# Macaron block with chunked attention and retention: a head's transposes, values and the bias a step or two later in the order of the work

## The chip, the cores and the metric

The kernel runs on one core of one Trainium2 chip. Time is device time in microseconds (us) of one execution, from the first to the last instruction and what lies around it. A shorter time is better. A tile (also a bank, where it lies in the accumulators' memory) is a buffer of 128 partitions.

## The reference

One layer over x of 256 x 2048 (f32): a half-step SwiGLU network, two mixers in parallel that are merged by sigmoid gates, a second half-step network and a last norm.

```
x = x + 0.5 * swiglu_ffn(rmsnorm(x), w_gate, w_up, w_down)          # d_ff = 5632
h = rmsnorm(x)
q_a,k_a,v_a, q_r,k_r,v_r, g_r, gate_a,gate_r = split(h @ w_in)
att = softmax(q_a k_a' * hd**-0.5 + bias[rel]) v_a                  # 8 heads of 128, chunks of 64, causal by chunk
ret = (rotary(q_r) rotary(k_r)' * decay) v_r, rms-normed a head     # 8 heads of 128
x = x + (sigmoid(gate_a)*(att @ w_out_att) + sigmoid(gate_r)*((silu(g_r)*ret) @ w_out_ret)) @ w_out
x = x + 0.5 * swiglu_ffn(rmsnorm(x), ...);  return rmsnorm(x)
```

The chunk rule only masks here: 256 rows are four chunks, and each sees its own and those before it.

## The kernel before

Every large product is a matmul in f32r, in three terms: both operands are split into a rounded part `hi` (ACT copies, line 122) and a rest `lo` (DVE subtracts, line 123), and PE adds hi x hi, lo x hi and hi x lo (lines 130 to 132, the tiles `acc`).

**Steps.** The kernel is a list of steps. A step takes one weight tile `raw` of 256 x 512 (512 KB, loaded by SP's queue) through twelve products of 512 columns: two halves of x, two blocks of rows, three terms. (In the gated parts, which use Strassen's scheme, tiles `z...`, a step has six.) Ahead of step c the weights of up to three steps further on are split. There are four places for split weights, so the split for step c+3 can start when the products of step c-1 are done.

**Work beside the products.** All else is put in a table of due times by hand: `later(n, fn)` puts fn n steps after the one that is being recorded, `at(step, fn)` puts it at a step. In a step the recording runs the split ahead first, then what is due, in the order in which it was put in the table, then the step's products. Each engine works through its own instructions in the order of recording. So what a due function has on PE stands ahead of the step's products, and what it has on DVE stands behind a split.

**Banks.** Products accumulate in tiles `acc` and `z` (three each). Work beside them uses the two side banks; a tile takes the one whose last reader was recorded first, and waits for that reader.

**The stretch around the change** lies between the last gated step and the merge. Step `mixed`, called m here, is the first of the value projection VR1 (m to m+7); then QR0 (to m+15), KR0 (to m+23), QR1 (to m+31), KR1 (to m+39), and the output products with `w_out_att` from m+40.

- *Bias.* `set_bias` at m-6 loads the relative bias, transposed, from a table in memory (`biasT`, two DMAs on POOL's queue). Four steps later, at m-2, `bias_natural` turns it on PE in four groups of four transposes (`psb`, line 326), each into a side bank and copied out by ACT (`bias`, line 331).
- *Attention*, head h, from m+4+4h: **scores** (PE `as`, lines 854 and 855; DVE adds the bias into `p`, line 862, and takes the maxima `m`), a step later **powers** (ACT's exponentials, line 876), in the third step **shares** (DVE divides, line 884), in the fourth **transposes** (PE `apt`, line 890, copied by ACT), and in the sixth **values** (PE `av`, lines 898 and 899; ACT copies `atth`, DVE subtracts `attl`, line 344). Each head shifts by four steps, so that the sixth step of one is the second of the next.
- *Retention's operands.* After QR0, KR0, QR1 and KR1, ACT copies the result out, DVE applies the rotary turn to its two halves in the first and second step after (`qr00r`, `qr01r` and so on, lines 815 to 818), and in the fourth PE transposes them (`qr0p`, `kr0p`, `qr1p`, `kr1p`, line 349) for ACT and DVE to copy (`qr0T` ...).
- *Retention*, heads 0 to 3 after KR0 and 4 to 7 after KR1: `RET_WAIT` steps after the projection the first head's **scores** (PE `rs`, lines 923 and 924; DVE multiplies by the decay, `rp`, lines 926 and 927), the next head's two steps later; **values** (PE `ro`, lines 936 to 938) two steps behind a head's scores; and behind the fourth head's values **finish** (ACT squares, DVE sums `ms`, POOL's power `rs`, DVE scales `rg`, line 954). Three steps later `ret.put` transposes the result (`retp`).
- *Merge.* The gates come back from memory as `siga` and `sigr` (POOL's queue, line 1010); DVE multiplies them with the output products (line 1027).

## Time and profile before

| | |
|---|---|
| median of 3 runs (lowest to highest) | 2120.16 us (2119.79 to 2121.63) |
| the profiled execution: time, span | 2121.39 us, 2119.6 us |
| PE busy, instructions | 2070.2 us (98%), 9256 |
| DVE, ACT, POOL busy | 1760.7, 1407.4, 273.3 us |
| mean granted PE clock | 0.995 |
| moved by DMA | 473.27 MB, 223 GB/s |

Engines: PE multiplies (PEld loads its weights), DVE is the vector engine, ACT the scalar one, POOL and SP issue DMAs among other things. A row of the timeline reads: start, length, engine, line, operation, tile written <- tiles read, shapes, count, and in brackets how long the engine was idle just before and what ended that. A row of the waits reads: who waited, for whom: total us, times, longest. The clock of a stretch is the share of full speed that PE was granted.

### The profile page before, as it was taken

The page shows a single profiled execution, that of the slowest core. Times are in us where ns is not written, and L with a number is a line of the kernel's source. Part 1 is how long each engine was busy: PE and PEld are TensorE (multiplying, and loading weights), DVE is VectorE, ACT ScalarE, POOL GpSimd, SP SyncE. Part 2 cuts the span into 40 slices and gives each one's busy share as a digit, 9 for nine tenths or more (in the row PEclk, how much of TensorE's full clock was granted, in tenths as well). Part 3 has the DMA queues.
Part 4 walks back from the last instruction along what each step waited for, and adds up shares of the span by engine and source line. Part 5 has one row for each costly group of instructions (what it writes and reads, how often), then busy time and mean ns, then how long its engine had stood idle before and what let it go on. Part 6 is the DMA issues. An engine that isn't in the chain of part 4 may idle for free.

```text
span 2119.6 us, 25816 instructions
## 1 busy us (share of the span) xinstructions
PE 2070.2 (98%) x9256; PEld 1692.1 (80%) x9256; DVE 1760.7 (83%) x1825; ACT 1407.4 (66%) x1734; POOL 273.3 (13%) x322
## 2 busy tenths in 40 slices
PE   8999999999999999999999999999999999999998
PEld 6788878878888888878777778887888878788886
DVE  6998889888997799888856567568889988898986
ACT  7677667777777766666654334556676677677775
POOL 1111211122111121012100000010121012110200
PEclk9999999999999999999999999999999999999999
DMA  8767886788668677789765645576787669766873
GB/s 299 199 216 231 261 231 196 234 253 258 188 228 268 230 225 221 241 267 295 224 206 159 193 149 177 186 228 177 236 273 222 196 220 276 223 203 228 280 209 129
DMA packets 219313, 473.27 MB, mean 223 GB/s; under 512 B 14816, under 2 KB 15568, under 8 KB 219184
## 3 DMA queue, kind: packets, MB, share of 16 engines
q1 hardware_dynamic: 161376, 310.42, 44.0%
q0 software_dynamic: 54752, 155.88, 27.4%
q10 hardware_dynamic: 3056, 5.32, 0.7%
q8 instruction: 72, 1.18, 0.2%
q14 instruction: 57, 0.47, 0.1%
HBM read 462.65 MB, written 8.91 MB: 222 GB/s over the span
## 4 chain that ended last, share of the span: by engine, by line
PE 75%; DVE 11%; issue 4%; ACT 4%; DMA 3%; ACTq 0%; POOL 0%; POOLq 0%; DVEq 0%
PE acc L131 14%; PE acc L132 14%; PE acc L130 14%; DVE lo L123 3%; DMA raw<-in_ffn_w_down_dram 2%; ACT hi L122 1%; DMA z992x<-in_ffn_w_gate_dram 1%; DMA raw<-in_w_in_dram 1%; PE z380a L130 0%; PE z128a L131 0%; PE z128a L130 0%; PE z380a L132 0%; PE z380a L131 0%; PE z684a L130 0%; PE z89a L131 0%
## 5 line engine op out<-in xcount | busy, mean ns | idle before, releaser
L123 DVE TENSOR_TENSOR lo<-raw,hi 128x1024 fp32r<-128x1024 f32 (+1 forms) x401 | 488.9, 1221 | 196.0 <-ACT hi L122 194.6
L122 ACT CAST hi<-raw 128x1024 fp32r<-128x1024 f32 (+1 forms) x401 | 419.1, 1048 | 247.3 <-PE acc L132 168.9
L730 ACT ACTIVATE acc<-xall 128x512 f32<-128x512 f32 x96 | 57.5, 599 | 8.4 <-DVE f1g L697 3.5
L733 ACT ACTIVATE xall<-acc 128x512 f32<-128x512 f32 x96 | 56.4, 587 | 4.6 <-PE acc L132 3.9
L130 PE MATMUL acc<-hi,mgh 128*128 128x512 f32 x128 | 50.2, 392 | 0.0
L132 PE MATMUL acc<-hi,mgl 128*128 128x512 f32 x128 | 49.9, 390 | 0.0
L131 PE MATMUL acc<-lo,mgh 128*128 128x512 f32 x128 | 49.9, 390 | 0.0
L131 PE MATMUL acc<-lo,nma01h 128*128 128x512 f32 x96 | 39.1, 407 | 2.3 <-DVE lo L123 2.3
L130 PE MATMUL acc<-hi,nma01h 128*128 128x512 f32 x96 | 39.9, 416 | 0.0
L130 PE MATMUL acc<-hi,nma00h 128*128 128x512 f32 x96 | 39.0, 406 | 0.0
L132 PE MATMUL acc<-hi,nma01l 128*128 128x512 f32 x96 | 38.3, 399 | 0.0
L131 PE MATMUL acc<-lo,nma00h 128*128 128x512 f32 x96 | 37.9, 395 | 0.3 <-DVE lo L123 0.3
L132 PE MATMUL acc<-hi,nma00l 128*128 128x512 f32 x96 | 37.6, 392 | 0.0
L130 PE MATMUL acc<-hi,nma10h 128*128 128x512 f32 x96 | 37.5, 391 | 0.0
L132 PE MATMUL acc<-hi,nma11l 128*128 128x512 f32 x96 | 37.5, 390 | 0.0
L131 PE MATMUL acc<-lo,nma11h 128*128 128x512 f32 x96 | 37.5, 390 | 0.0
L131 PE MATMUL acc<-lo,nma10h 128*128 128x512 f32 x96 | 37.4, 390 | 0.0
L130 PE MATMUL acc<-hi,nma11h 128*128 128x512 f32 x96 | 37.4, 390 | 0.0
L132 PE MATMUL acc<-hi,nma10l 128*128 128x512 f32 x96 | 37.4, 390 | 0.0
L132 PEld LDWEIGHTS acc<-hi,mgl 128*128 128x128 f32 x128 | 24.0, 188 | 4.9
L130 PEld LDWEIGHTS acc<-hi,mgh 128*128 128x128 f32 x128 | 24.1, 188 | 4.9
L131 PEld LDWEIGHTS acc<-lo,mgh 128*128 128x128 f32 x128 | 24.1, 188 | 4.8
(6130 smaller groups left out, 7158.5 us busy)
## 6 DMA issues: line engine op xcount, KB each, us to landing
raw<-in_ffn_w_down_dram SPq DMA_DIRECT2D x176, 512.0 KB, 6.3
raw<-in_w_in_dram SPq DMA_DIRECT2D x96, 512.0 KB, 4.5
raw<-in_ffn_w_up_dram SPq DMA_DIRECT2D x32, 512.0 KB, 8.2
raw<-in_w_out_dram SPq DMA_DIRECT2D x32, 512.0 KB, 3.7
raw<-in_ffn_w_gate_dram SPq DMA_DIRECT2D x31, 512.0 KB, 4.6
raw<-in_w_out_att_dram SPq DMA_DIRECT2D x16, 512.0 KB, 4.1
raw<-in_w_out_ret_dram SPq DMA_DIRECT2D x16, 512.0 KB, 3.8
z380x<-in_w_in_dram POOLq DMA_DIRECT2D x8, 512.0 KB, 7.9
```

Source lines behind the costliest of these rows:

```text
L122: nc.scalar.copy(hi[:, p, :], raw[:, p, :])
L123: nc.vector.tensor_sub(lo[:, p, :], raw[:, p, :], hi[:, p, :].bitcast(F32))
L130: nc.tensor.matmul(acc, ahi, whi, start=first, stop=False, **more)
L131: nc.tensor.matmul(acc, ahi, wlo, start=False, stop=False, **more)
L132: nc.tensor.matmul(acc, alo, whi, start=False, stop=last, **more)
L730: nc.scalar.activation(acc, xs[t][:, cols], AF.Copy, scale=2.0)
L733: nc.scalar.activation(xs[t][:, cols], acc, AF.Copy, scale=0.5)
```

## The change

Numbers in the table of due times move, and nothing else:

```
-RET_WAIT = (14, 6)
+RET_WAIT = (14, 5)
...
-        return (0, scores), (1, powers), (2, shares), (3, transposes), (5, values)
+        return (0, scores), (1, powers), (2, shares), (4, transposes), (6, values)
...
-                later(wait + 2 * i + 2 * s, stage)
-        later(wait + 2 * 4, finish)
+                later(wait + 2 * i + 3 * s, stage)
+        later(wait + 2 * 4 + 1, finish)
...
-    at(mixed - 6, set_bias)
+    at(mixed - 4, set_bias)
```

A head's transposes now stand in step m+8+4h, ahead of the next head's scores, and its values in m+10+4h. Retention's values and finish stand a step later for heads 0 to 3 (values m+40 to m+46, finish m+46, `retp` m+49); for heads 4 to 7 the scores stand a step earlier (m+44 to m+50), values and finish where they stood (m+47 to m+53). The bias is turned at m instead of m-2.

In the rows below the numbers in names are buffer numbers; they differ between the two kernels where tiles are made in another order, and mean nothing else. First PE at head 0's transposes (`apt`) and head 1's scores (`as`), one piece of the difference:

```order
 L131 MATMUL acc_1_9003<-lo_9053,nma11h 128x512
 L132 MATMUL acc_1_9003<-hi_9052,nma11l 128x512
-L890 MATMUL apt_9147<-id_sb,p_9079 128x128 x3
 L130 MATMUL acc_0_9002<-hi_9070,nma01h 128x512
 L131 MATMUL acc_0_9002<-lo_9071,nma01h 128x512
@@ -4624,4 +4623,5 @@
 L131 MATMUL acc_1_9003<-lo_9071,nma11h 128x512
 L132 MATMUL acc_1_9003<-hi_9070,nma11l 128x512
+L890 MATMUL apt_9168<-id_sb,p_9079 128x128 x3
 L854 MATMUL as_9173<-ka0T,qa0T 128x256
 L855 MATMUL as_9173<-ka0T,qa0T 128x128
```

The transposes have moved behind twelve more products and now stand directly ahead of the next scores.

Then DVE beside head 3, where it also turns the second half of QR0 (`qr01r`); `attl` is what head 2's values leave to DVE, `p` and `l` are head 3's shares. Before:

```order
L123 TENSOR_TENSOR lo_9419<-raw_9274,hi_9418 128x1024
L344 TENSOR_TENSOR attl_9209<-av_9424,atth_9208 128x256
L815 TENSOR_TENSOR qr01r<-qr_9371,cos_sb 128x4x64
L816 TENSOR_TENSOR qr01u<-qr_9371,sin_sb 128x4x64
...
L818 TENSOR_TENSOR qr01r<-qr01r,qr01u 128x4x64
L123 TENSOR_TENSOR lo_9452<-raw_9304,hi_9451 128x1024
L882 RECIPROCAL l<-l 128x2
L884 TENSOR_SCALAR p_9387<-p_9387,l 128x256
```

After:

```order
L123 TENSOR_TENSOR lo_9419<-raw_9269,hi_9418 128x1024
L815 TENSOR_TENSOR qr01r<-qr_9366,cos_sb 128x4x64
L816 TENSOR_TENSOR qr01u<-qr_9366,sin_sb 128x4x64
...
L818 TENSOR_TENSOR qr01r<-qr01r,qr01u 128x4x64
L123 TENSOR_TENSOR lo_9447<-raw_9304,hi_9446 128x1024
L344 TENSOR_TENSOR attl_9229<-av_9452,atth_9228 128x256
L882 RECIPROCAL l<-l 128x2
L884 TENSOR_SCALAR p_9387<-p_9387,l 128x256
```

`attl` has moved from ahead of the turn to behind it and behind a split. The shares have the same work ahead of them as before. PE's `qr0p` for that half, which took the bank of head 3's transposes before, now takes the bank that `attl` reads.

Last, the bias on ACT, where it copies what PE has turned, and retention's finish on DVE. ACT before and after:

```order
L982 ACTIVATE z531c_8895<-z531c_8895 128x512
L986 DMA gr_105<-z531c_8895 128x512
L122 CAST hi_8941<-raw_8780 128x1024
L331 COPY bias_8947<-psb_8949 128x512
L331 COPY bias_8947<-psb_8955 128x512
L331 COPY bias_8948<-psb_8961 128x512
L331 COPY bias_8948<-psb_8967 128x512
L122 CAST hi_8981<-raw_8794 128x1024
```

```order
L982 ACTIVATE z531c_8891<-z531c_8891 128x512
L986 DMA gr_105<-z531c_8891 128x512
L122 CAST hi_8941<-raw_8780 128x1024
L122 CAST hi_8953<-raw_8794 128x1024
L122 CAST hi_8965<-raw_8822 128x1024
L331 COPY bias_8971<-psb_8973 128x512
L331 COPY bias_8971<-psb_8979 128x512
L331 COPY bias_8972<-psb_8985 128x512
L331 COPY bias_8972<-psb_8991 128x512
```

The four copies have moved behind two more splits. On DVE, from the finish of heads 0 to 3 on, after the change (before, the row ran: `rg`, `rp` of head 4, two `lo`, `rp` of head 5, two `siga`, `lo`, `retl`):

```order
L954 SCALAR_TENSOR_TENSOR rg_10292<-ro_10092,rs,gr_9375 128x128 x4
L926 TENSOR_TENSOR rp_10300<-rs_10297,decay_9510 128x256
L927 TENSOR_TENSOR rp_10300<-rs_10297,decay_9510 128x128
L123 TENSOR_TENSOR lo_10316<-raw_10154,hi_10315 128x1024
L1027 TENSOR_TENSOR siga_9984<-acc_0_10230,siga_9984 128x512
L1027 TENSOR_TENSOR siga_9984<-acc_1_10231,siga_9984 128x512
L123 TENSOR_TENSOR lo_10341<-raw_10175,hi_10340 128x1024
L926 TENSOR_TENSOR rp_10349<-rs_10346,decay_9510 128x256
L927 TENSOR_TENSOR rp_10349<-rs_10346,decay_9510 128x128
L123 TENSOR_TENSOR lo_10367<-raw_10213,hi_10366 128x1024
L344 TENSOR_TENSOR retl_10376<-retp_10377,reth_10375 128x4x128
```

The `rp` rows here are heads 5 and 6; head 4's now stands ahead of the finish. The second half of `retp` uses the bank of head 6's scores, and so stands behind the second `rp` here.

## The prediction

> **What bounds the kernel now.** I read the page's engine shares first, then the waits of PE, then the places behind them in the order of time.

> ```profile
> span 2119.6 us, 25816 instructions
> PE 2070.2 (98%) x9256; PEld 1692.1 (80%) x9256; DVE 1760.7 (83%) x1825; ACT 1407.4 (66%) x1734; POOL 273.3 (13%) x322
> ```

> PE is busy for 98% of the span, so a gain has to come from the 49 us in which it is not, or from products that run slowly. The waits of PE, of which I show five rows (in total, times, longest), say where the idle time lies:

> ```profile
> PE acc L131 <- DVE lo L123: 9.6, 21, 0.7
> PE apt L890 <- DVE p L884: 9.3, 8, 2.2
> PE psb L326 <- ACT bias L331: 2.7, 1, 2.7
> PE ro L936 <- DVE rp L926: 2.1, 1, 2.1
> PE kr1p L349 <- ACT kr1T L784: 0.7, 1, 0.7
> ```

> The second to fourth are what the change moves. Eight times, once a head, the transposes `apt` wait for the shares that DVE made in the same step before. In the order of time an ordinary head and head 3 look like this:

> ```profile
> 1094.58 0.39 PE L132 MATMUL acc<-hi,nma11l 128*128 128x512 f32 x1
> 1095.92 0.52 PE L890 MATMUL apt<-id_sb,p 128*128 128x128 f32 x3 [0.96 <-DVE p L884]
> 1109.20 0.52 PE L890 MATMUL apt<-id_sb,p 128*128 128x128 f32 x3 [0.48 <-DVE p L884]
> ...
> 1134.86 0.39 PE L132 MATMUL acc<-hi,nma11l 128*128 128x512 f32 x1
> 1137.40 0.52 PE L890 MATMUL apt<-id_sb,p 128*128 128x128 f32 x3 [2.15 <-DVE p L884]
> 1137.76 0.91 PE L349 MATMUL qr0p<-id_sb,qr00r 128*128 128x128 f32 x4
> 1139.83 0.63 PE L131 MATMUL acc<-lo,nma01h 128*128 128x512 f32 x1
> 1140.25 0.63 PE L132 MATMUL acc<-hi,nma01l 128*128 128x512 f32 x1
> ```

> Two readings. A product is drawn 0.39 long while the next starts 0.23 after it, so each shown wait is 0.16 short: 1094.58 to 1095.92 is 1.34, less 0.23 is 1.11, where the row says 0.96. And after the 2.15 wait the products start 0.42 apart instead of 0.23. The granted clock says the same by stretch (length, busy times of PE, PEld, DVE, ACT and POOL, clock, DMA):

> ```profile
> 1066.00:1076.00 10.00, 7.32 (x35) 6.16 (x34) 5.14 (x7) 5.89 (x9) 0.00 (x0) 0.83 0.44 134
> 1126.00:1143.00 17.00, 14.85 (x66) 12.11 (x65) 11.58 (x27) 6.76 (x12) 0.53 (x1) 0.90 0.59 183
> 1143.00:1157.00 14.00, 13.53 (x66) 11.04 (x64) 7.14 (x14) 6.86 (x12) 0.53 (x1) 1.00 0.55 155
> 1157.00:1174.00 17.00, 14.85 (x66) 12.15 (x65) 11.58 (x27) 6.57 (x12) 0.00 (x0) 0.90 0.50 151
> 1237.00:1250.00 13.00, 10.95 (x57) 8.99 (x56) 9.40 (x21) 3.93 (x6) 2.03 (x2) 1.00 0.41 129
> ```

> A clock of 0.90 over 17 us is 1.7 us lost, and 0.83 over 10 us is 1.7 too: one drop costs 1.7 us beside its wait. It follows the waits of 2.15 (the 9.3 of the wait row is 0.96 + 4 x 0.48 + 3 x 2.15; heads 3 and 5 lie in the two stretches of 0.90) and of 2.69. The ones of 0.48 and, in the last stretch, of 2.06 leave the clock at 1.00. The DMA engines are busy for 0.41 to 0.59 of these stretches, so weights do not bound them.

> [...]

> **The change part by part.** It adds and removes no instruction and no DMA. Every step still has twelve products; steps are numbered from m, the step `mixed`.

> *Transposes one step later.* The shares stand in step m+6+4h, the transposes then in m+8+4h, a whole step of products further. The wait rows give 9.3 + 8 x 0.16 = 10.6 us, and three clock drops (heads 3, 5 and 7, whose waits are 2.15) give 3 x 1.7 = 5.1. Both go, 15.7 in all, if nothing else is late in those steps. (For head 7 the third drop is taken like the other two.) Scores, transposes and values themselves cost the same wherever they stand.

> *What is late next.* Beside heads 3, 5 and 7 DVE also turns retention's queries or keys (`qr`, `kr`):

> ```profile
> 1125.57 0.59 PE L854 MATMUL as<-ka0T,qa0T 128*128 128x256 f32 x2
> 1127.43 1.23 DVE L123 TENSOR_TENSOR lo<-raw,hi 128x1024 fp32r<-128x1024 f32 x1 [3.05 <-ACT hi L122]
> 1128.57 0.68 DVE L862 SCALAR_TENSOR_TENSOR p<-as,bias 128x128 f32<-128x128 f32 x3
> 1128.97 0.59 PE L898 MATMUL av<-p,va 128*128 128x256 f32 x2
> 1129.88 0.42 DVE L815 TENSOR_TENSOR qr00r<-qr,cos_sb 128x256 f32<-128x256 f32 x1
> 1131.90 1.22 DVE L123 TENSOR_TENSOR lo<-raw,hi 128x1024 fp32r<-128x1024 f32 x1
> 1133.03 0.42 DVE L344 TENSOR_TENSOR attl<-av,atth 128x256 fp32r<-128x256 f32 x1
> 1133.37 0.42 DVE L815 TENSOR_TENSOR qr01r<-qr,cos_sb 128x256 f32<-128x256 f32 x1
> 1135.37 1.23 DVE L123 TENSOR_TENSOR lo<-raw,hi 128x1024 fp32r<-128x1024 f32 x1
> 1136.71 0.55 DVE L884 TENSOR_SCALAR p<-p,l 128x256 f32<-128x256 f32 x2
> ```

> DVE runs here without a gap. The transposes of the turned queries (`qr0p`) keep their step, m+19. Their second half needs a side bank, and in the new order that bank was the values' (`av`, now in m+18), freed by `attl`. Counted from step m+16 (1125.57): `lo` starts at 1.86, the scores' work lasts 1.31 after it, then turn 2.02, `lo` 1.13, turn 2.00, `lo` 1.14, and `attl`, now behind all of them, starts at 10.6 and ends at 11.0. PE is at m+19 after a step with transposes and scores (3.40 by 1125.57 to 1128.97, and 0.4 for three transposes at the 0.1 that eight `psb` or `retp` below take each, with 0.1 in the products behind), a bare step (12 x 0.227 = 2.72) and one with values (3.4 like the scores): 9.9, and 10.3 after the first half. It waits until 11.15: 0.86. Three times: 2.6 lost. Bounds: nothing, if the bank is free sooner, or 0.86 + 1.7 each if the clock drops; I take 0.86, as it is nearest to the 0.96 row, after which the clock held. The moved transposes of head 3 then find their shares long made (11.7 against 14.4), and so do the scores behind them find the `qr0T` copy (13.5).

> *Values one step later* wait for ACT's copy two steps before, as now. No other instruction waits for `attl` before the first output product, after m+40.

> *Bias two steps later.* Four groups of transposes (`psb`) share two banks, so the third waits for ACT's first copy:

> ```profile
> 1066.20 1.03 PE L326 MATMUL psb<-id_sb,biasT 128*128 128x128 f32 x8
> 1069.92 1.97 PE L326 MATMUL psb<-id_sb,biasT 128*128 128x128 f32 x8 [2.69 <-ACT bias L331]
> 1071.54 0.78 PE L130 MATMUL z531a<-hiz53132s,nma11h 128*128 128x512 f32 x1
> ...
> 1068.34 1.04 ACT L122 CAST hi<-raw 128x1024 fp32r<-128x1024 f32 x1 [0.45 <-ACT z531c L982]
> 1069.29 1.07 ACT L331 COPY bias<-psb 128x512 f32<-128x512 f32 x2
> ```

> Sixteen transposes cost 1.6 (eight are drawn 1.03 long, the last one's tail under what follows: 0.8); 1066.20 to 1071.54 is 5.3, so 3.7 is lost, and 0.8 more in slow products: 4.6. Afterwards PE passes two short steps first (2 x 1.36) and begins `psb` at 1068.92. ACT is late there, from `z531c` on: its `hi` at 1068.34 is now followed by two more, 0.95 apart, so the first copy starts at 1071.2 and the third group at 1071.8, and the products at 1072.7. That loses 2.2, so 2.4 is gained. The wait, 1.9 as a row would show it, is nearest to the 2.06 that left the clock alone; with a drop 0.7 is gained, and without any wait 4.6. The two `biasT` loads keep their place on POOL's queue, behind `z531x` and ahead of `gr`. The gate loads (`siga`, `sigr`) further back there wait for the heads' tiles, which come free a step later, and are first used after m+43. SP's queue holds only weights, in the order that it had.

> *Retention.* Head 4's scores move ahead of the finish of heads 0 to 3 on DVE, and its values no longer wait for it:

> ```profile
> 1236.23 0.38 PE L936 MATMUL ro<-vr,rp 128*128 128x128 f32 x2
> 1245.24 0.49 PE L936 MATMUL ro<-vr,rp 128*128 128x128 f32 x2 [2.06 <-DVE rp L926]
> 1249.43 1.03 PE L349 MATMUL retp<-id_sb,rg 128*128 128x128 f32 x8
> ...
> 1244.77 0.42 DVE L926 TENSOR_TENSOR rp<-rs,decay 128x256 f32<-128x256 f32 x1
> 1248.27 0.69 DVE L1027 TENSOR_TENSOR siga<-acc,siga 128x512 f32<-128x512 f32 x1
> ```

> 2.06 + 0.16 = 2.2 go. The finish ends 8.5 us into its step (1236.23 to 1244.77). After it DVE now has `rp` of head 5 (0.5), a `lo` (1.1), two `siga` (0.6 each), a `lo` (1.1) and `rp` of head 6 (0.7): 13.2. PE reaches the `retp` transposes in m+49, three steps on, at 4.1 + 3.5 + 3.4 = 11.0 (the 4.19 of 1245.24 to 1249.43 is a step with both values and scores; one alone takes 3.4 to 3.5), and their second half, which needs head 6's bank, at 12.0. It waits 1.3. `kr1p` waits 0.2 longer, as its scores now stand right ahead. Net 0.7 gained; bounds 2.2 (no wait) and -1.0 (a clock drop there). The next products in the finished banks (m+48, second half) start at 4.1 + 3.5 + 0.6 + 1.4 = 9.6 and need them at 8.7.

> **The sum:** 10.6 + 5.1 - 2.6 + 2.4 + 0.7 = 16.2 us. The profiled execution took 2121.39, 1.2 above the median 2120.16; from the one it gives 2105.2, from the other 2104.0. I say 2104.5.

> **The rivals.** *The clock drops at the new waits too.* A 2.06 wait spared it and a 2.15 wait did not, one against four cases, so length alone may not decide. Five drops at 1.7 leave 16.2 - 8.5 = 7.7: 2113. [...] Chance 0.12, for a few or all of them.

> *The splits become the bound.* The largest wait row, `acc` for `lo`, averages 9.6/21 = 0.46; at each of the 32 steps under the heads this would take 14.7 back, and the time would be 2119, no change. Against it: DVE is busy 11.58 of 17 us even beside a turn, and splits stand three steps ahead. Chance 0.05.

> *Slower: the side banks.* Transposes and the next head's scores now take both side banks in one step, and the second needs the bank that `attl` frees. If `attl` came later than two steps, 3.40 + 2.72 = 6.1 us, after its values, seven heads would wait some 2.3 and lose 1.7 of clock: 28 lost against 16 gained, 2132. Today it ends 4.5 us after them (1128.97 to 1133.45), beside a turn and, as worked out, 4.5 in the new order. Chance 0.03.

> **How the numbers follow.** The forecast, with some of its terms off, has 0.80 (2099 to 2110). The range runs from 2099, almost all terms at their better bounds (15.7 + 4.6 + 2.2 = 22.5 would be 2098), to 2113, the first rival. A measurement of this kernel can tell 0.2%, 4 us, from no change: faster takes the forecast and the first rival, 0.92; the splits' case gives same 0.05; the banks slower 0.03.

> **What would show it.** Right: no `apt` row in PE's waits; in its place `qr0p`, `kr0p` and `qr1p` three times 0.5 to 1.1 on `attl`; `psb` about 1.9; `ro` gone, `retp` about 1.3; the granted clock 1.00 from 1085 to 1300. Wrong: a clock under 1.00 there, new rows of `as` or `av`, or more waits of `acc` for `lo` in this stretch.

## The result and the profile after

The changed kernel takes 2104.67 us (median of 6 runs, 2102.1 to 2106.27), beside 2120.86 for the kernel before on the same chip: a ratio of 0.9923 with a 95% interval of 0.991 to 0.9936, which is 13.6 to 19.1 us less. Five more runs on another occasion gave 0.9925 (0.9911 to 0.9938). The forecast was 2104.5, with a sum of 16.2. The profiled execution took 2105.12; its page begins:

```profile
span 2103.4 us, 25824 instructions
PE 2065.5 (98%) x9256; PEld 1688.7 (80%) x9256; DVE 1761.1 (84%) x1825; ACT 1408.4 (67%) x1734; POOL 273.8 (13%) x322
```

The work is the same; 16.2 us of the span are gone. The waits of PE (who waited, for whom: total, times, longest):

```profile
PE acc L131 <- DVE lo L123: 8.3, 19, 0.8
PE psb L326 <- ACT bias L331: 1.9, 1, 1.9
...
PE retp L349 <- DVE rp L927: 1.0, 1, 1.0
...
PE kr1p L349 <- ACT kr1T L784: 0.7, 1, 0.7
PE qr1p L349 <- DVE attl L344: 0.6, 1, 0.6
PE qr0p L349 <- DVE attl L344: 0.6, 1, 0.6
PE kr0p L349 <- DVE attl L344: 0.6, 1, 0.6
```

The rows `apt` (9.3) and `ro` (2.1) are gone. In their place stand those that the prediction named: three times 0.6 for `attl`, 1.0 for retention's `rp`, and `psb` at 1.9. The row of `kr1p` has not grown. Four of the stretches that were shown of before (length, busy times of PE, PEld, DVE, ACT and POOL, clock, DMA):

```profile
1066.00:1076.00 10.00, 8.14 (x41) 6.59 (x40) 7.00 (x8) 7.55 (x11) 0.00 (x0) 0.90 0.56 178
1126.00:1143.00 17.00, 16.40 (x81) 13.54 (x80) 13.52 (x35) 7.94 (x15) 0.53 (x1) 1.00 0.62 186
1157.00:1174.00 17.00, 16.41 (x81) 13.55 (x81) 11.97 (x27) 7.17 (x13) 0.53 (x1) 1.00 0.57 159
1237.00:1250.00 13.00, 11.97 (x64) 9.87 (x62) 8.78 (x13) 4.33 (x5) 0.00 (x0) 1.00 0.51 161
```

Beside the heads the clock is now 1.00. Around the bias it is still 0.90: a drop follows the wait of 1.85. The timeline at the bias, at the first turned queries and at retention's `retp`:

```profile
1072.84 1.15 PE L326 MATMUL psb<-id_sb,biasT 128*128 128x128 f32 x8 [1.85 <-ACT bias L331]
...
1132.91 0.60 PE L349 MATMUL qr0p<-id_sb,qr00r 128*128 128x128 f32 x4
1133.64 0.41 DVE L344 TENSOR_TENSOR attl<-av,atth 128x256 fp32r<-128x256 f32 x1
1134.11 0.66 PE L349 MATMUL qr0p<-id_sb,qr01r 128*128 128x128 f32 x4 [0.60 <-DVE attl L344]
...
1238.29 0.60 PE L349 MATMUL retp<-id_sb,rg 128*128 128x128 f32 x4
1239.92 0.66 PE L349 MATMUL retp<-id_sb,rg 128*128 128x128 f32 x4 [1.03 <-DVE rp L927]
```

**Where the 16.2 came from.** Three marks cut both executions in the same places: a product that waits for a split well ahead of the bias, head 0's scores, and the first transposes `mgp` of the merge. (Head 0's scores of before are at 1085.96.) Before:

```profile
1036.11 0.50 PE L131 MATMUL acc<-lo,nma01h 128*128 128x512 f32 x1 [0.60 <-DVE lo L123]
1085.96 0.59 PE L854 MATMUL as<-ka0T,qa0T 128*128 128x256 f32 x2
1290.44 0.82 PE L349 MATMUL mgp<-id_sb,sigr 128*128 128x128 f32 x6
```

After:

```profile
1037.16 0.50 PE L131 MATMUL acc<-lo,nma01h 128*128 128x512 f32 x1 [0.58 <-DVE lo L123]
1086.33 0.59 PE L854 MATMUL as<-ka0T,qa0T 128*128 128x256 f32 x2
1276.52 1.03 PE L349 MATMUL mgp<-id_sb,sigr 128*128 128x128 f32 x8
```

| stretch | before | after | gained | the prediction's terms |
|---|---|---|---|---|
| start to the first mark | 1036.11 | 1037.16 | -1.05 | 0 |
| to head 0's scores (bias) | 49.85 | 49.17 | 0.68 | 2.4 |
| to the merge (heads, retention) | 204.48 | 190.19 | 14.29 | 15.7 - 2.6 + 0.7 = 13.8 |
| to the end | 829.16 | 826.88 | 2.28 | 0 |

So the stretch that the change touches gave 15.0, not 16.2. The other 1.2 lie where both kernels are the same, and are scatter between executions: over the thirteen profiles of the two kernels and their variants (the clock probe left out) the start to the first mark varies by 2.8 us and the way from the merge to the end by 3.6, though none of their edits touches either.

### The profile page after: what moved, and what is told of

It reads as the page before. It is cut to its first block, busy times and chain, and to the rows that moved or that the text cites. A ratio compares the mean times of both kernels' runs of the same rounds, so it can differ in the third digit from the quotient of the medians.

```text
span 2103.4 us, 25824 instructions
## 1 busy us (share of the span) xinstructions
PE 2065.5 (98%) x9256; PEld 1688.7 (80%) x9256; DVE 1761.1 (84%) x1825; ACT 1408.4 (67%) x1734; POOL 273.8 (13%) x322
## 4 chain that ended last, share of the span: by engine, by line
PE 77%; DVE 11%; issue 4%; ACT 4%; DMA 3%; ACTq 0%; POOL 0%; POOLq 0%; DVEq 0%
PE acc L131 15%; PE acc L132 14%; PE acc L130 14%; DVE lo L123 2%; DMA raw<-in_ffn_w_down_dram 2%; ACT hi L122 1%; DMA z992x<-in_ffn_w_gate_dram 1%; DMA rawz24323r<-in_ffn_w_up_dram 1%; ACT xall L733 0%; PE z128a L131 0%; PE z800a L131 0%; PE z205a L130 0%; PE z380a L130 0%; PE z128a L130 0%; PE z800a L130 0%
## 5 line engine op out<-in xcount | busy, mean ns | idle before, releaser
L123 DVE TENSOR_TENSOR lo<-raw,hi 128x1024 fp32r<-128x1024 f32 (+1 forms) x401 | 487.2, 1217 | 176.5 <-ACT hi L122 174.7
L122 ACT CAST hi<-raw 128x1024 fp32r<-128x1024 f32 (+1 forms) x401 | 418.9, 1048 | 230.0 <-PE acc L132 143.7
L130 PE MATMUL acc<-hi,mgh 128*128 128x512 f32 x128 | 50.1, 392 | 0.0
L132 PE MATMUL acc<-hi,mgl 128*128 128x512 f32 x128 | 49.8, 389 | 0.0
L131 PE MATMUL acc<-lo,mgh 128*128 128x512 f32 x128 | 49.8, 389 | 0.0
L131 PE MATMUL acc<-lo,nma01h 128*128 128x512 f32 x96 | 38.0, 396 | 1.6 <-DVE lo L123 1.6
L130 PE MATMUL acc<-hi,nma00h 128*128 128x512 f32 x96 | 38.9, 405 | 0.0
L131 PE MATMUL acc<-lo,nma00h 128*128 128x512 f32 x96 | 38.4, 400 | 0.3 <-DVE lo L123 0.3
L130 PE MATMUL acc<-hi,nma01h 128*128 128x512 f32 x96 | 38.5, 401 | 0.0
L132 PE MATMUL acc<-hi,nma00l 128*128 128x512 f32 x96 | 38.0, 396 | 0.0
L130 PE MATMUL acc<-hi,nma10h 128*128 128x512 f32 x96 | 37.7, 393 | 0.0
L131 PE MATMUL acc<-lo,nma10h 128*128 128x512 f32 x96 | 37.6, 392 | 0.0
L132 PE MATMUL acc<-hi,nma01l 128*128 128x512 f32 x96 | 37.6, 391 | 0.0
L132 PE MATMUL acc<-hi,nma10l 128*128 128x512 f32 x96 | 37.5, 390 | 0.0
L132 PE MATMUL acc<-hi,nma11l 128*128 128x512 f32 x96 | 37.4, 390 | 0.0
L130 PE MATMUL acc<-hi,nma11h 128*128 128x512 f32 x96 | 37.4, 390 | 0.0
L131 PE MATMUL acc<-lo,nma11h 128*128 128x512 f32 x96 | 37.4, 389 | 0.0
L132 PEld LDWEIGHTS acc<-hi,mgl 128*128 128x128 f32 x128 | 24.0, 188 | 4.9
L130 PEld LDWEIGHTS acc<-hi,mgh 128*128 128x128 f32 x128 | 24.0, 188 | 4.9
L131 PEld LDWEIGHTS acc<-lo,mgh 128*128 128x128 f32 x128 | 24.0, 188 | 4.9
```

What stands on the lines that cost most here:

```text
L122: nc.scalar.copy(hi[:, p, :], raw[:, p, :])
L123: nc.vector.tensor_sub(lo[:, p, :], raw[:, p, :], hi[:, p, :].bitcast(F32))
L130: nc.tensor.matmul(acc, ahi, whi, start=first, stop=False, **more)
L131: nc.tensor.matmul(acc, ahi, wlo, start=False, stop=False, **more)
L132: nc.tensor.matmul(acc, alo, whi, start=False, stop=last, **more)
```

## The experiments

Each time stands beside the kernel before, run on the same chip in the same series. A time shows differences of a few us; smaller ones are read between the marks above, in the profiles.

| kernel | median | before | ratio (95%) |
|---|---|---|---|
| heads only | 2108.41 | 2120.37 | 0.994 (0.9928 to 0.9953) |
| bias only | 2119.24 | 2120.37 | 0.9991 (0.9983 to 1.0) |
| retention only | 2119.06 | 2120.37 | 0.999 (0.9981 to 0.9999) |
| turned apart | 2116.98 | 2120.37 | 0.9985 (0.9977 to 0.9994) |
| new, bias spread | 2101.31 | 2119.35 | 0.9914 (0.9899 to 0.9928) |
| new, values early | 2101.43 | 2119.35 | 0.9915 (0.99 to 0.993) |
| new, all waits away | 2095.69 | 2119.35 | 0.9887 (0.9871 to 0.9904) |
| new, again | 2107.2 | 2121.99 | 0.9925 (0.9911 to 0.9938) |
| heads only, again | 2105.96 | 2121.99 | 0.9925 (0.9913 to 0.9937) |
| values early, again | 2102.43 | 2121.99 | 0.9906 (0.9892 to 0.9919) |
| bias spread, again | 2102.81 | 2121.99 | 0.991 (0.9896 to 0.9923) |

### The three parts, one at a time

Heads only, against the kernel before:

```
-        return (0, scores), (1, powers), (2, shares), (3, transposes), (5, values)
+        return (0, scores), (1, powers), (2, shares), (4, transposes), (6, values)
```

> The heads' part alone (transposes in the fourth step behind the scores, values in the sixth); retention and bias as before. By the prediction's terms 10.6 + 5.1 - 2.6 = 13.1 less than before (2120.9), 2107.8; by the new trace's marks (the rope waits cost 0.8 each) 13.3, 2107.6. Rival: the parts lean on each other, and retention's old places collide with head 7's later values: a gain under 11. The bias wait stays 2.7 with its slow products, and the wait of ro for rp stays 2.1.

It gained 12.0, and 16.0 when it was run again beside the new kernel, 14.0 on average, near the 13.1 of the prediction's terms. The heads' part is nearly the whole change. Its two profiles show no row of `apt`, and `psb` at 2.7 and `ro` at 2.1 as before.

Bias only:

```
-    at(mixed - 6, set_bias)
+    at(mixed - 4, set_bias)
```

> The bias part alone (turned at m instead of m-2). The prediction's term: 2.4 less, if the clock holds through a wait of about 1.9. By the new trace's marks (49.85 us from one mark to head 0's scores before, 49.17 after) 0.7 less, with some eight products 0.42 apart behind the wait. The profile tells them apart: slow products behind the second group of transposes or none. The time can hardly (0.7 of 2121 is 0.03%).

1.1 less by the medians, with an interval that reaches no change (0.0 to 3.6). Its wait of `psb` is 1.86, as long as in the new kernel, but no slow product follows: the clock is 1.00 in the 3.41 us behind it, where the new kernel has 0.50. The same instructions at the bias, the same wait, another outcome.

Retention only:

```
-RET_WAIT = (14, 6)
+RET_WAIT = (14, 5)
...
-                later(wait + 2 * i + 2 * s, stage)
-        later(wait + 2 * 4, finish)
+                later(wait + 2 * i + 3 * s, stage)
+        later(wait + 2 * 4 + 1, finish)
```

> The retention part alone. The prediction's term is 0.7 less, the new trace's marks say 1.0 (2.2 gone, 1.2 for the transposes retp that now wait for rp). Rival: with the heads in their old places the transposes of head 7 and retention's first steps share the banks in another way and a wait of 0.5 to 2 appears: no gain or a loss of 1.

1.3 less by the medians (0.2 to 4.0). The row of `ro` is gone and that of `retp` stands at 1.0, as in the new kernel. The rival's new wait beside head 7 is not there. The three parts give 14.0 + 1.1 + 1.3 = 16.4, the whole change 15.5 (the mean of 16.2 and 14.8): they add within what these times can tell.

### When the clock dropped

Head 3's wait of 2.15 and its fellows cost a drop each, the 2.06 of `ro` none, and the new kernel's 1.85 one: length alone was wrong. The first try moved the transposes that stood behind those waits, in the kernel before:

```
-            to_transposed(key, b, srcs, 4)
+            to_transposed(key, b, srcs, 4 if (key, b) == ("kr", 1) else 7)
```

> The kernel before, with one number changed: the transposes of the turned queries and keys (qr0p, kr0p, qr1p) three steps later, so that they no longer stand right behind the transposes of heads 3, 5 and 7, which wait 2.15. Theory A: what counts for the clock is the stretch without a product, waits and transposes together; before, it was 2.15 + 0.16 + 1.9 = 4.2 there; now it is 2.15 + 0.16 + 0.3 = 2.6, little more than the 2.2 that the clock stood, so three drops go: 3 x 1.7 = 5.1 less, 2115.8, with the three waits of 2.15 still there. Theory B: the length of the wait alone counts, 2.15 is over the limit: three drops stay, 2120.9. Theory C: a window that runs free decides by its phase: one or two of the three stay.

3.4 faster (1.3 to 4.9), between the theories, and its profile contradicts A and B. The three waits are 2.14 each, with only three transposes behind them. Heads 3 and 5 drop and head 7 does not, and the 2.05 of `ro`, which had been spared before, drops. The edit did one thing more than was meant: the waits of 0.48 at heads 4 and 6 are gone as well (the row of `apt` reads 8.3 in 6 times, where before it was 9.3 in 8), which is worth 2 x 0.64 = 1.3. From head 0's scores to the merge the profile takes 203.06, 1.4 less than before, with three drops in that stretch in both. Each pair of rows is a stretch of 3.41 us and the next one; the first number behind the length is PE's busy time, the clock stands third from the end:

```profile
1134.03:1137.44 3.41, 1.27 (x8) 0.80 (x7) 3.37 (x9) 1.04 (x1) 0.00 (x0) 1.00 0.55 153
1137.44:1140.85 3.41, 3.41 (x11) 2.65 (x10) 0.59 (x1) 0.48 (x1) 0.00 (x0) 0.50 0.79 218
...
1195.48:1198.89 3.41, 1.74 (x9) 1.52 (x10) 2.62 (x5) 1.14 (x2) 0.00 (x0) 1.00 0.53 175
1198.89:1202.30 3.41, 3.41 (x16) 2.82 (x15) 0.69 (x1) 1.05 (x1) 0.00 (x0) 1.00 0.58 199
1239.85:1243.26 3.41, 1.38 (x11) 1.33 (x11) 2.89 (x8) 1.04 (x1) 0.49 (x1) 1.00 0.01 2
1243.26:1246.67 3.41, 3.41 (x10) 2.73 (x10) 2.08 (x4) 0.00 (x0) 0.00 (x0) 0.50 0.66 213
```

The stretches are not chosen freely. Cut in this way, the clock of this profile reads 0.50 or 1.00, each drop lasts 3.41 us, and the four drops begin 0, 20, 29 and 51 times 3.413 us behind the first (174.08 us for the 51, from 1069.18 to 1243.26). I read the stretches as places of a grid, of which a drop here fills one. The kernel before, read in this way (three of its four drops, and the spared wait of `ro`):

```profile
1134.51:1137.92 3.41, 1.26 (x9) 0.83 (x8) 3.38 (x8) 1.04 (x1) 0.00 (x0) 1.00 0.48 152
1137.92:1141.33 3.41, 3.41 (x14) 2.79 (x12) 1.16 (x2) 1.06 (x2) 0.00 (x0) 0.50 0.78 235
...
1168.64:1172.05 3.41, 3.41 (x14) 2.88 (x13) 1.24 (x2) 1.06 (x2) 0.00 (x0) 0.50 0.82 227
...
1199.36:1202.77 3.41, 3.41 (x14) 2.89 (x13) 1.26 (x2) 1.06 (x2) 0.00 (x0) 0.50 0.77 235
1243.73:1247.14 3.41, 1.90 (x13) 1.76 (x14) 3.41 (x8) 0.54 (x1) 0.00 (x0) 1.00 0.00 0
1247.14:1250.55 3.41, 3.41 (x21) 2.91 (x20) 2.43 (x5) 0.92 (x1) 0.00 (x0) 1.00 0.72 237
```

Two readings. The wait of `ro` lay across two places, with PE busy for 2.87 in the one (1240.32 to 1243.73) and for 1.90 in the other, and the clock stayed at 1.00 behind both; and the waits of heads 3, 5 and 7 end 30.80 and 30.74 us apart (1137.40, 1168.20, 1198.94), where nine places are 30.72, so that they fell on nearly the same phase, with PE busy for 1.26 in the place of each, and dropped together. They were one observation, not three. With the transposes moved, the same three waits come every 30.06 us (1137.04, 1167.10 and 1197.15), so each falls 0.66 earlier in its place, and the third is spared, with 1.74 busy.

The probe asks the grid and the limit at many places. From the output products on it adds, in every third step, either a row of transposes or a gap:

```
+    def transposes_in_a_row(n):            # n = 16 to 64
+        ps = side_tile("probe")
+        for i in range(n):
+            nc.tensor.transpose(ps[:, (i % 4) * P : (i % 4 + 1) * P], id_sb, id_sb)
+    def idle(n):                           # n = 0 to 11
...
+        nc.scalar.copy(t, ps[:, :P])
+        for i in range(n):
+            nc.scalar.copy(t, t)
+        nc.tensor.transpose(ps[:, P : 2 * P], t, id_sb)
```

> The new kernel with PE work added that nothing needs, in every third step from the output products on, in turn a row of 16 to 64 transposes without a wait (1.6 to 6.4 us) and two transposes with 1 to 12 copies on ACT between them (an idle stretch of some 0.7 to 4 us). Only the clock is asked; the time grows by the added work. Theory A: PE's idle time in a stretch of 3.41 us of a fixed grid decides, transposes count as work; a share of idle over about 0.58 costs the next stretch half its clock: no row of transposes drops, not even one of 6.4, and each drop begins a whole number of 3.41 us from the others, behind a stretch that is idle for more than 0.58. Theory B: transposes count as idle: all rows of 64 and most of 40 and 48 drop. Theory C: the length of one wait decides, whatever its phase: all gaps over some length drop and none under it.

The run agrees with theory A, but with idle shares of 0.54 to 0.56 between drops and none, not 0.58. The probe ran once, and only its clock is read. Forty-three times the clock falls, and each fall lies a whole number of places behind the first (the last, at 2578.30, 368.0 places behind 1322.20). The extremes, in order: the first drop with the place behind it, the least PE work that was spared, one of the two with the most that was not, and the last drop.

```profile
1318.79:1322.20 3.41, 0.87 (x5) 0.43 (x3) 2.67 (x3) 2.46 (x7) 0.00 (x0) 1.00 0.38 127
1322.20:1325.61 3.41, 2.45 (x11) 2.36 (x12) 0.47 (x1) 1.66 (x5) 0.00 (x0) 0.50 0.70 245
1325.61:1329.03 3.42, 3.42 (x10) 2.65 (x9) 0.92 (x2) 0.35 (x1) 0.00 (x0) 0.50 0.03 10
1984.39:1987.80 3.41, 1.51 (x7) 1.29 (x8) 1.48 (x2) 1.69 (x7) 0.00 (x0) 1.00 0.70 226
1987.80:1991.21 3.41, 3.41 (x19) 2.84 (x19) 1.93 (x2) 2.54 (x3) 0.55 (x1) 1.00 0.45 162
2322.31:2325.72 3.41, 1.56 (x8) 1.07 (x7) 2.83 (x3) 1.80 (x4) 0.00 (x0) 1.00 0.77 240
2325.72:2329.13 3.41, 3.41 (x10) 2.63 (x9) 1.80 (x3) 1.09 (x2) 1.22 (x1) 0.50 0.40 92
2574.89:2578.30 3.41, 0.89 (x5) 0.75 (x6) 3.41 (x4) 2.27 (x8) 1.09 (x1) 1.00 0.21 77
2578.30:2581.71 3.41, 3.41 (x10) 2.64 (x9) 1.49 (x2) 1.04 (x1) 0.13 (x1) 0.50 0.79 118
```

I laid the grid through 14 profiled executions, from 20 us to the last products, some 8500 places with the clock full. 60 were followed by a drop, and in each PE's drawn busy time was at most 1.56 of the 3.41; in none of the others was it under 1.51. Between 1.51 and 1.56, where the drawn ends are uncertain, both occur; that is 44 to 46% of a place. What sets it no profile here shows.

The first drop lasts two places, as 12 of the 43 do: PE's drawn busy time in the first half-clocked place was at most 2.63 in those twelve and at least 2.77 in the others. Both lie above the 1.51 to 1.56 between a drop and none. In the other kernels' profiles all 17 drops last one place.

Theory C falls: a wait of 3.17 that lay across two places, with PE busy for 2.10 and 1.55 in them, was spared, and one of 1.85 inside one place, with 1.56, dropped. All 27 waits over 3.2 dropped.

```profile
1713.18 0.33 PE L1176 MATMUL gap<-id_sb,chain 128*128 128x128 f32 x1 [3.17 <-ACT chain L1175]
2324.47 0.33 PE L1176 MATMUL gap<-id_sb,chain 128*128 128x128 f32 x1 [1.85 <-ACT chain L1175]
```

Theory B falls: no row of transposes dropped, the longest included.

```profile
1870.95 7.15 PE L1167 MATMUL probe<-id_sb 128*128 128x128 f32 x64
...
1874.36:1877.77 3.41, 3.41 (x34) 3.41 (x33) 0.00 (x0) 0.00 (x0) 0.00 (x0) 1.00 0.00 0
1877.77:1881.18 3.41, 3.41 (x18) 2.85 (x17) 0.00 (x0) 0.31 (x1) 0.00 (x0) 1.00 0.02 5
```

The row starts at 1870.95 and the product behind it at 1877.85: the clock was at 1.00 ahead of these f32 transposes and stayed there for their 6.9 us.

That the phase is a matter of the single execution is shown by kernels that were profiled twice. The new kernel again, and heads only again, both without an edit:

> The new kernel again, beside the next three on one chip. What it does against the kernel before should repeat: 16.2 less (13.6 to 19.1 by the first interval).

> The heads' part alone again. First time 12.0 less than before, where the marks of the new trace give 10.6 - 2.4 and the drops that the three heads had. If the parts simply add, it lies 1.0 (retention) and 0.7 to 2.4 (bias) behind the new kernel: 1.7 to 3.4 slower. If the parts lean on each other, it lies over 4 behind it.

The times are in the table: 14.8 less than before, and 16.0. So on this chip heads only came out 1.2 ahead of the new kernel, where 1.7 to 3.4 behind it was expected; over all their runs, chips mixed, it is 1.6 behind (2106.7 in 10 runs, 2105.1 in 11). The times cannot tell so little. The profiles can: from head 0's scores to the merge heads only takes 191.15 and 191.08, the new kernel 190.19 and 190.23, so retention adds 0.9 to the heads' part where 1.0 was expected, and the parts do not lean on each other. Heads only has its bias wait at the old place; its first profile, then its second:

```profile
1071.14 1.14 PE L326 MATMUL psb<-id_sb,biasT 128*128 128x128 f32 x8 [2.68 <-ACT bias L331]
1066.76:1070.17 3.41, 1.70 (x12) 1.29 (x10) 2.82 (x3) 2.01 (x3) 0.00 (x0) 1.00 0.06 25
1070.17:1073.58 3.41, 2.44 (x15) 2.12 (x16) 1.76 (x3) 2.48 (x5) 0.00 (x0) 1.00 0.80 227
```

```profile
1069.04 1.44 PE L326 MATMUL psb<-id_sb,biasT 128*128 128x128 f32 x8 [2.69 <-ACT bias L331]
1066.35:1069.76 3.41, 0.72 (x7) 0.65 (x7) 2.35 (x3) 2.67 (x5) 0.00 (x0) 1.00 0.48 147
1069.76:1073.17 3.41, 3.41 (x11) 2.83 (x10) 0.54 (x2) 1.24 (x3) 0.00 (x0) 0.50 0.75 235
```

One program, one wait of 2.7: across two places, with PE busy for 1.70 and 2.44 in them, it cost nothing more; inside one place, with 0.72 busy, it cost a drop. The new kernel did the same: a drop behind its wait of 1.85 in the first profile (1.55 busy in one place), none behind 1.86 in the second (3.11 and 1.84 in two).

### Taking away the waits that are left

Values early, against the new kernel:

```
-        ... (4, transposes), (6, values)
+        ... (4, transposes), (5, values)
```

> The new kernel with a head's values back in the fifth step behind its scores, one step behind its transposes. If the prediction's account of the bank is right, attl is ahead of the rotary turn again, the second halves of qr0p, kr0p and qr1p find their bank free, and 3 x 0.8 = 2.4 goes: 2102.3. Rival: one step is too short for ACT's copy of the transposes (it ends 2.2 behind them beside an ordinary head), and values wait for it at the heads beside a turn: 0.5 to 1 each, 2104 to 2106.

> Values one step behind the transposes, again. Its trace shows no wait of qr0p, kr0p or qr1p and no new one, so it should be 3 x 0.8 = 2.4 faster than the new kernel on the same chip. If it is the same within 1, the rope waits were paid for elsewhere.

Both halves of `qr0p` now follow each other at once, as do those of `kr0p` and `qr1p`, and no row of `av` has come:

```profile
1130.17 0.60 PE L349 MATMUL qr0p<-id_sb,qr00r 128*128 128x128 f32 x4
1130.60 0.60 PE L349 MATMUL qr0p<-id_sb,qr01r 128*128 128x128 f32 x4
```

The two series give 17.9 and 19.6 less than before, where the new kernel gives 16.2 and 14.8. On one chip the medians stand 4.8 apart; over all runs (8 and 11) 2.7. From head 0's scores to the merge the two profiles take 187.78 and 187.70, beside 190.19 and 190.23: 2.4 to 2.5 less, as expected. So the account of the bank was right, and the values' second step was not needed: ACT's copy is ready one step behind the transposes.

Bias spread, against the new kernel:

```
-        for h in range(0, HEADS, 2):
+        for h in range(4 * b, 4 * b + 4, 2):
...
-        later(4, lambda: bias_natural(bt))
+        for b in range(HEADS // 4):
+            later(4 + b, lambda b=b: bias_natural(bt, b))
```

> The new kernel with the bias turned in two parts, heads 0 to 3 at m and heads 4 to 7 at m+1, so that the third group of transposes finds its bank copied out a step of products earlier. The wait of psb (1.85 + 0.16) goes, and the drop that followed it in some executions (half of the six of the new kernel showed a mean clock of 0.998 instead of 0.999): 2.0 + 0.5 x 1.7 = 2.9 less than the new kernel's 2104.7, 2101.8. Rival: ACT is late by as much a step later too, and the wait moves to m+1: no gain, 2104.7.

> The bias in two steps, again. Its trace shows no wait of psb, so 2.0 less than the new kernel on the same chip, and 1.7 more in those executions in which the new kernel's clock dropped behind that wait: 2.0 to 3.7 less in the median.

The row of `psb` is gone in both profiles, and no other row has come in its place. 18.0 and 19.2 less than before; beside the new kernel 4.4 less on the same chip, a little over the 2.0 to 3.7 expected, and 3.5 less over all runs (9 and 11). From the first mark to head 0's scores the profiles take 45.76 and 45.52: 2.2 to 2.4 less than the new kernel's profile without a drop (47.93), 3.4 to 3.7 less than the one with it (49.17). So one step was enough for ACT's copies.

All together, against the new kernel (values stay where the change put them, the turned operands move instead), beside the bias as above:

```
-            to_transposed(key, b, srcs, 4)
+            to_transposed(key, b, srcs, 6 if b == 0 else {"qr": (4, 5), "kr": (3, 4)}[key])
...
-            later(3, lambda: [ret.put(b, t, srcs[t]) for t in range(NT)])
+            for t in range(NT):
+                later(3 + (2 * t if b == 0 else 0), lambda t=t: ret.put(b, t, srcs[t]))
```

A pair of numbers gives each half its own step.

> The new kernel with every wait that it left or added taken away: the bias in two steps, qr0p and kr0p two steps later, where no other side tile is made, the halves of qr1p and kr1p in two steps each, the halves of head 0 to 3's retp two steps apart. From the new kernel's 2104.7: 2.9 (bias) + 2.4 (turned queries and keys) + 1.2 (retp) + 0.8 (kr1p) = 7.3 less, 2097.4. Rival: the second half of qr0p now waits for the next head's scores to be read by DVE, and gives 0.5 to 1 back each time: 2099. If the time falls by under 3, the waits were covered by something else, the weights or the splits.

2095.69: 23.7 less than before (20.4 to 27.3), and 7.5 or 8.9 less than the new kernel by the differences of its two series, with 7.3 expected. It beats both kernels. In the 215 us from 1085 on PE is drawn busy without a gap (one under the 0.16 by which a product is drawn too long would not show):

```profile
1085.00:1300.00 215.00, 215.00 (x1044) 180.18 (x1043) 146.61 (x268) 99.40 (x144) 8.81 (x13) 1.00 0.57 191
```

## Why the prediction was right, and where it was not

- *Transposes one step later, 10.6:* right. All eight waits are gone, and nothing new waits in those steps.
- *Three drops, 5.1:* gone, but the reason was wrong. The prediction tied a drop to the wait's length, and counted three cases for what was one phase; a wait of 1.85 inside one place of 3.41 us dropped, and the 2.06 across two did not. What the heads' drops are worth on average is seen in the mean granted clock: 0.9955 over 43 runs of before, 0.9980 over the 10 of heads only. 0.0025 of 2120 is 5.3 us, three drops of 1.7. So the heads' waits of before did drop in most executions, and 5.1 was a fair size.
- *The turned queries and keys, -2.6:* right in place and nearly in size. From the first half of `qr0p` to the second are 1.20, of which four transposes take 0.40: 0.80 each, where the prediction had 0.86: 2.4 in all.
- *Bias, 2.4:* mis-sized; this is the one term that was far off. The wait came out as predicted (1.85 for 1.9). "Nearest to the 2.06 that left the clock alone" did not decide: in the profiled execution the place 1070.51 to 1073.92 had PE busy for 1.55, the clock dropped, and 0.68 was gained, the prediction's own lower value of 0.7. In the second profile the wait fell otherwise, and its way from the same mark to head 0's scores, 47.93, is 1.9 shorter than before; that of bias only, also without a drop there, is 47.59, 2.3 shorter. A chance between 0.7 and 2.4 would have been the right term.
- *Retention, 0.7:* nearly right, 1.0 by the waits and 0.9 between the marks. 2.2 went; `retp` waits 1.23 (1.63 between its halves, less 0.40) where 1.3 was said; `kr1p` waits no longer than before, where 0.2 was added.
- *The sum:* the marks give 15.0. That it came within 0.2 of the median is in part luck: the 1.7 too much in the bias is made up by 0.5 from heads and retention and 1.2 of scatter.
- *The rivals:* that the clock drops at the new waits came true for the bias alone; the waits of 0.6 to 1.0 did not, and every place with a drop behind it in the 14 profiles was idle for 1.85 or more (3.41 less 1.56). The splits did not become the bound (the row of `acc` fell from 9.6 to 8.3), and the side banks held: no row of `as`, and `attl` beside head 3 ends at 1134.05, the next head's scores start at 1137.68.

## What to carry to other kernels

A wait that moves off PE can be taken at its row's length plus the 0.16 by which the product ahead of it is drawn too long here (0.39 drawn, 0.23 to the next start), and the wait that replaces it is found by following whose bank the next tile gets. When DVE's or ACT's answer is a step late, move the instruction that waits by one step and leave those behind it where they find their bank free (values early), or put its halves in two steps (bias spread): both cost nothing here and removed the wait whole. In these profiles a wait on PE was dearer by 1.7 us where it left one place of 3.41 us idle for more than 1.90 (3.41 less 1.51; from 1.85 on both occur), and one program did so in one execution and not in another. So price such waits by chance, over several executions, and count waits that lie nearly a whole number of places apart, like the 30.80 and 30.74 us here, as one.
